# One pass over the attention scores, staggered merging, and a re-ordered set of queues in a two-block float32 transformer kernel

## The chip, the cores and the metric
The kernel runs on one core of one Trainium2 chip. The metric is device time in microseconds (us) from the start to the end of one execution; the median of the runs is what counts.

## The reference
A sequence of 512 tokens with 1024 channels passes two models, one after the other, in float32. The first has two layers, each with a mixer and a gated MLP with a causal convolution of width 3, each half with a norm before and a norm behind, and with shift, scale and gate columns from a modulation vector (`mod = silu(c) @ mod_w[l]`, six pieces of 1024 for each layer). The mixer of layer 0 is a convolution block (two products, a depthwise convolution of width 31, a LayerNorm over channels and a swish). That of layer 1 is differential attention:

```python
s = q . k * scale + bias;  s = where(rel >= 0, s, -inf);  p = softmax(s)      # for both halves c of a head
a = p[:, :, 0] - lam * p[:, :, 1];  o = a @ v
o = rms_norm(o, subln_g) * (1 - lambda_init);  y = o.reshape(S, 1024) @ w_o
```

The second model has one block: an input product to all of the attention inputs and gates, a sparse attention (an indexer picks 128 keys for a query; 8 heads share k and v), a second causal attention from low-rank latents (8 heads, rotary part of 32), two branch products merged with gates, `x + merged @ w_out`, and an MLP with a squared relu, then a final norm.

## The kernel before
Every large product is done as three float32r products (`mm3`, L204 to L207): high part by high part, low by high, high by low. So each piece of weights that comes from DRAM (`wr`) is cast by ScalarE to its high part (`wh`, L137), and the low part is a subtraction (`wl`, L139) on VectorE or, where `b.lo_pool` says so, on GpSimd; `LO_POOL` gives every how many-th piece by stage. Activations are split likewise (`hh`, `hl`, L350 and L351). Tokens lie in 4 tiles of 128 (`tok`); a transposition of a tile is 8 products of 128x128 (`transp`, L334).

Each engine runs its instructions in the order of the code. `Builder.ahead(n)` loads and splits the next n pieces (`la` pieces split ahead, `ld` loaded ahead), `get` takes one, and `tick` takes one step of a background generator, above all of `mod_chunk` (L243: 8 multiply-adds of 128x1024, called macc, for one piece of `mod`; then products with ones, L259 for columns or L266 for broadcast rows). `HELD` names pieces whose last part is done at a fixed later place.

The places that the change touches, in order of the program:
- **Start** (`keep_busy`, `m_pe`, loop over `k` at L840 to L884). Products by 128 columns `hh` with `w1` (L859) alternate with one-column products for the first `mod` columns (L744). `h_evac` (L772, L773) makes `hh` of the next step from a transposition and the `mcol` columns (L279).
- **LayerNorm** before `w2` (`ln_tok`, L978 to L1006): `ln_norm` (L969) makes `zn`, `ln_put` the transposition and its evacuation (L976). `down8` (L461 to L501) is a product with a 1024x1024 matrix for 4 token tiles, in 2 halves of 8 steps each, with the norm chain of a tile (`chain`) put between the steps of the next.
- **MLPs of the first model**: `run_ffn` starts the background list `bg`.
- **Attention of layer 1**: `proj(hd)` makes q and k of a head (`kq`, L1192 to L1194). An item is a head and a query tile `(hd, qb)`, with n = 128(qb+1) keys. `attn1_s` (L1197 to L1235) does two score products (`sc`, c = 0, 1), then on VectorE a maximum of the part without bias (L1213), an add-and-maximum of the last 256 columns with the bias (L1214), then on ScalarE an exp of each part (L1220, L1222), and sums and differences in `comb` (L1229 to L1233). `attn1_t` transposes the weights (`aT`, L1241), `attn1_v` multiplies with v (L1249) and writes `o` (L1251). When head 7 of a tile is done, GpSimd raises 8 columns to the power -1/2 (L195) and VectorE scales all of `o` (L1302, 128x1024); the scaled tile is transposed for `wo`'s `down8`, which runs among the last items and behind them. `MULT` and `AGE` count items until the scaling and the transposition.
- **Second block**: the input projection (units, rope on 32 rows, `kh`), the indexer's selection, and the items of both attentions (`mla_s` L1574 to L1603, `dsa_s` L1605 to L1620), with gate units and branch-b units as fillers between items. `cmaj` (L1666 to L1673) turns a finished tile to channels for the branch product. `LALD2` is set by `deeper()` before the first branch-b unit.
- **Merge** (L1721 to L1732): 8 branch-a units; after each second one the pair of gates is added (L1729), halved and split (`mgh` L1730, `mgl` L1731); then `wout` by `down8`.

## Time and profile before

| | us |
|---|---|
| median of 3 runs (lowest, highest) | 2028.94 (2028.92, 2034.42) |
| the profiled execution | 2029.45 |
| its span in the trace | 2027.7 |
| TensorE (PE) busy | 1960.3, 97% |
| VectorE (DVE) busy | 1258.3, 62% |
| ScalarE (ACT) busy | 827.6, 41% |
| GpSimd (POOL) busy | 138.7, 7% |
| mean granted TensorE clock | 0.988 |

A share of busy time is a mean over stages; the time of a program like this is lost where PE waits. The timeline of PE has 53 waits of 0.15 us or more. Two kinds of loss can be read: a wait itself, in brackets behind an instruction with what ended it, and a stretch in which the granted clock is at the lower of its two levels (1.2 GHz instead of 2.4), which the view by windows shows as PEclk near 0.5.

### The profile page before, as it was taken

How to read it: one execution, taken by the hardware profiler on the slowest of the kernel's cores; microseconds unless marked ns; L12 is line 12 of the kernel's file. 1: busy time of each engine (PE TensorE's matmuls, PEld its weight loads, DVE VectorE, ACT ScalarE, POOL GpSimd, SP SyncE). 2: the span in 40 equal slices, each digit the busy share in tenths (PEclk: the TensorE clock that was granted, in tenths of full speed). 3: DMA queues.
4: the chain of work that ended last, by engine and by line, in shares of the span. 5: the costliest groups of instructions: out<-in, count | busy, mean ns of one | idle time of the engine just before them, and what ended most of it. 6: DMA issues, size and time to landing. Idle time of an engine off the chain costs nothing. (4 is left out here: it accounts for less than half of the span.)

```text
span 2027.7 us, 25858 instructions
## 1 busy us (share of the span) xinstructions
PE 1960.3 (97%) x9722; PEld 1616.4 (80%) x9725; DVE 1258.3 (62%) x2406; ACT 827.6 (41%) x1675; POOL 138.7 (7%) x99
## 2 busy tenths in 40 slices
PE   9999999999999999889999999998999999999998
PEld 6889788777887877678888887867777878888887
DVE  5779677777855565767666623678686746433432
ACT  3312454443424456744444413554445435322421
POOL 1001000000000111210000000122212100000000
PEclk8999999999999999999999999999999999999999
DMA  9455146434675211312932323311114442332221
GB/s 358 133 206 196 74 151 224 156 125 138 244 265 175 82 46 64 142 59 92 256 104 84 125 73 137 121 57 53 42 52 130 152 161 90 124 125 84 82 94 42
DMA packets 85417, 259.47 MB, mean 128 GB/s; under 512 B 9429, under 2 KB 21117, under 8 KB 85290
## 3 DMA queue, kind: packets, MB, share of 16 engines
q1 hardware_dynamic: 77802, 232.63, 34.1%
q10 hardware_dynamic: 7488, 25.17, 3.3%
q8 instruction: 76, 1.25, 0.3%
q14 instruction: 51, 0.42, 0.1%
HBM read 243.04 MB, written 23.64 MB: 132 GB/s over the span
## 5 line engine op out<-in xcount | busy, mean ns | idle before, releaser
L205 PE MATMUL up<-hh,wh 128*128 128x512 f32 (+1 forms) x1232 | 456.4, 370 | 3.4 <-ACT wh L137 1.7
L207 PE MATMUL up<-hh,wl 128*128 128x512 f32 (+1 forms) x1232 | 453.8, 368 | 4.0 <-DVE wl L139 3.9
L206 PE MATMUL up<-hl,wh 128*128 128x512 f32 (+1 forms) x1232 | 452.6, 367 | 0.2
L139 DVE TENSOR_TENSOR wl<-wr,wh 128x1024 fp32r<-128x1024 f32 (+2 forms) x257 | 311.8, 1224 | 174.1 <-ACT wh L137 146.7
L137 ACT CAST wh<-wr 128x1024 fp32r<-128x1024 f32 (+2 forms) x308 | 307.9, 1019 | 183.1 <-DMA wr<-in_w_all_dram 99.8
L207 PEld LDWEIGHTS up<-hh,wl 128*128 128x128 f32 x1232 | 232.0, 188 | 47.5 <-DVE wl L139 9.2
L205 PEld LDWEIGHTS up<-hh,wh 128*128 128x128 f32 x1232 | 232.0, 188 | 46.2 <-ACT wh L137 3.5
L206 PEld LDWEIGHTS up<-hl,wh 128*128 128x128 f32 x1232 | 232.1, 188 | 40.2 <-issue 1.5
L205 PE MATMUL acc<-wh,ih 128*128 128x512 f32 x608 | 237.4, 390 | 0.0
L206 PE MATMUL acc<-wl,ih 128*128 128x512 f32 x608 | 236.8, 389 | 0.2 <-DVE wl L139 0.2
L207 PE MATMUL acc<-wh,il 128*128 128x512 f32 x608 | 236.7, 389 | 0.0
L139 POOL TENSOR_TENSOR wl<-wr,wh 128x1024 fp32r<-128x1024 f32 (+1 forms) x51 | 108.0, 2125 | 975.3 <-ACT wh L137 912.2
L206 PEld LDWEIGHTS acc<-wl,ih 128*128 128x128 f32 x608 | 114.1, 188 | 24.3 <-DVE wl L139 0.9
L207 PEld LDWEIGHTS acc<-wh,il 128*128 128x128 f32 x608 | 114.1, 188 | 23.8
L205 PEld LDWEIGHTS acc<-wh,ih 128*128 128x128 f32 x608 | 114.1, 188 | 23.6
L243 DVE SCALAR_TENSOR_TENSOR macc<-mraw,cact,macc 128x1024 f32<-128x1024 f32 x74 | 95.4, 1289 | 6.6 <-DMA mraw<-in_mod_w_dram 6.0
L1071 ACT CAST ih<-fc 128x512 fp32r<-128x512 f32 x44 | 37.9, 860 | 142.5 <-DVE fc L1063 142.5
L1039 ACT ACTIVATE fc<-up,cols 128x512 f32<-128x512 f32 x88 | 68.2, 775 | 36.0 <-PE up L207 36.0
L1044 DVE SCALAR_TENSOR_TENSOR fc<-up,cols,fc 128x384 f32<-128x384 f32 (+3 forms) x176 | 72.7, 478 | 4.1 <-ACT fc L1039 4.1
L205 PE MATMUL unit<-hh,wh 128*128 128x512 f32 x152 | 72.7, 479 | 0.7 <-ACT kh L1448 0.6
L1055 ACT ACTIVATE fc<-fc 128x512 f32<-128x512 f32 x44 | 27.8, 632 | 102.6 <-DVE fc L1044 61.6
L1072 DVE TENSOR_TENSOR il<-fc,ih 128x512 fp32r<-128x512 f32 x44 | 39.8, 904 | 40.8 <-ACT ih L1071 40.8
(336 smaller groups left out, 3110.3 us busy)
## 6 DMA issues: line engine op xcount, KB each, us to landing
wr<-in_w_all_dram SPq DMA_DIRECT2D x282, 512.0 KB, 3.7
mraw<-in_mod_w_dram SPq DMA_DIRECT2D x80, 512.0 KB, 4.9
xd<-x ACTq DMA_DIRECT2D x20, 512.0 KB, 2.6
x<-xd ACTq DMA_DIRECT2D x20, 512.0 KB, 5.8
mraw<-in_w_all_dram SPq DMA_DIRECT2D x16, 512.0 KB, 9.6
wr<-in_w_all_dram SPq DMA_DIRECT2D x17, 256.0 KB, 2.6
wr<-in_w_all_dram SPq DMA_DIRECT2D x8, 384.0 KB, 8.8
sk<-fd SPq DMA_DIRECT2D x6, 512.0 KB, 15.7
```

The costliest lines, as they stand in the source:

```text
L137: self.nc.scalar.copy(hi, raw)
L139: (self.nc.gpsimd if pool else self.nc.vector).tensor_tensor(out=lo, in0=raw, in1=hi, op=ALU.subtract)
L205: mm(ps, lh, rh, start=start, stop=False)
L206: mm(ps, lh, rl, start=False, stop=False)
L207: mm(ps, ll, rh, start=False, stop=stop)
L243: nc.vector.scalar_tensor_tensor(out=acc, in0=raws[k], scalar=s, in1=acc, op0=ALU.mult, op1=ALU.add)
L1039: nc.scalar.activation(out=o, in_=ps, func=AF.Identity, scale=dw[:, 88 + j:89 + j], bias=dwb[:, j:j + 1])
L1044: nc.vector.scalar_tensor_tensor(out=a, in0=e, scalar=dw[:, w + j:w + j + 1], in1=a, op0=ALU.mult, op1=ALU.add)
L1055: nc.scalar.activation(out=o, in_=o, func=AF.Silu)
L1071: nc.scalar.copy(hi, o)
L1072: nc.vector.tensor_sub(lo, o, hi)
```

## The change
1. **One pass over scores.** The bias tiles of attention 1 become [128, 512] for a head, zero in the first half; the add-and-maximum runs over all n columns, the maximum of the unbiased part is gone, and one exp serves a half of the item instead of two. The second block's causal attention does the same with a wide mask. The order lists have 65 instructions less on VectorE and 64 less on ScalarE.
2. **LO_POOL** goes from (2, 0, 2, 1, 0) to (0, 0, 0, 1, 0): 15 low parts in the stage of w_v and attention 1 and 6 in the second block's input projection go from GpSimd to VectorE. The eight rope copies to `kh` on GpSimd become four on VectorE.
3. **End of attention 1.** Heads 6 and 7 go query tile by query tile. Six heads of a tile are scaled when head 6 is done (128x768), the last two at age 1 (128x256). Within `wo` the norms' roots are taken on GpSimd (`power_on`) and not by ScalarE's Sqrt.
4. **Constant first products**: the last parts of three pieces of `mod` (m14, m13, m15: two times 8 one-column products for each of 2 parts, and 2 products with ones) go from the first MLP's down stage to fillers behind `proj(7)`.
5. **LayerNorm**: the transposition of tile 0 is put before the norm of tile 1; tiles 2 and 3 and the transposition of tile 1 go to step 5 of `w2`'s `down8`.
6. **Start**: `WARM` (32, 5) becomes (38, 2), with one more warm product after each 4 of the first group; for k = 0 `ahead(2)` moves behind `h_evac(1)`.
7. **PAUSE**: six empty ticks before the background list in both MLPs of the first model.
8. **Second block**: other `SEL_RATE`; `cmaj` of the causal attention at age 5 instead of 3; each bias load of the sparse attention one item earlier; `la`, `ld` grow by one for each branch-b unit; the merge's low part is issued behind the next unit, its last pair is merged singly; `wout`'s first tile does k < 6 of both halves first; `reload` one tile at a time.

```diff
-LO_POOL = (2, 0, 2, 1, 0)
+LO_POOL = (0, 0, 0, 1, 0)
-MULT = 4
+MULT = (1, 1, 1, 1)
-AGE = (9, 11, 6, 10, 14, 12, 21, 12)
-SEL_RATE = (1.4, 1, 0.6, 0.4, 1.0, 1.3, 1.3, 1.0, 1.2)
+AGE = (7, 11, 6, 8, 12, 12, 21, 12)
+SEL_RATE = (1.0, 1.4, 0.6, 0.4, 1.0, 1.3, 1.3, 1.0, 1.2)
-HELD = [(0, 2), (0, 4)]
-WARM = (32, 5)
+HELD = [(0, 2), (0, 4), (1, 4), (1, 3), (1, 5)]
+WARM = (38, 2)
+PAUSE = 6
...
@@ rstd2
-        if self.phase:
+        if self.phase or self.power_on:
...
@@ down8
+            cut = 0 if tok else last
+            todo = [(half, k) for half in range(2) for k in range(8 - cut)]
+            todo += [(half, k) for half in range(2) for k in range(8 - cut, 8)]
...
@@ start
-    for _ in m_pe(*START_GROUPS[0]):
-        pass
+    for i, _ in enumerate(m_pe(*START_GROUPS[0])):
+        if i % 4 == 3:
+            keep_busy(idle, 1)
...
-        b.ahead(2)
+        if k:
+            b.ahead(2)
...
             lo_k = h_evac(k + 1, h_t(k + 1))
+        b.ahead(2)
...
@@ ln_tok
+            ln_put(0)
             ln_norm(1)
-            ln_put(0)
...
-            ln_norm(2)
-            ln_put(1)
-            b.reload()
-            ln_norm(3)
...
+        if i == 5:
+            ln_next()
...
@@ run_ffn
-        b.bg += bg
+        b.bg += [('pause', iter(range(PAUSE)))] + bg
...
@@ attn1_s
-            if nf:
-                nc.vector.reduce_max(m[:, c:c + 1], sc[c][:, :nf], axis=AX.X)
-            nc.vector.tensor_tensor_reduce(out=pt[:, c, nf:n], in0=sc[c][:, nf:n], in1=bts, scale=1.0,
...
+            nc.vector.tensor_tensor_reduce(out=pt[:, c, :n], in0=sc[c][:, :n], in1=bt[hd][:, 512 - n:], scale=1.0,
+                                           scalar=-3.0e38, op0=ALU.add, op1=ALU.max, accum_out=m[:, c:c + 1])
...
+            nc.scalar.activation(out=pt[:, c, :n], in_=pt[:, c, :n], func=AF.Exp, bias=nm[:, c:c + 1],
+                                 accum_out=tot[:, c:c + 1])
...
@@ done
+        if hd == 5:
+            orr[tok] = b.rstd_pool(oss[tok][:, 0:6], 128, 6)
+        if hd == 6:
+            scale_heads(tok, 0, 6)
...
-        orr[tok] = b.rstd_pool(oss[tok], 128, 8)
+        orr[tok] = b.rstd_pool(oss[tok][:, 6:8], 128, 2)
...
-    fillers = [proj(hd) for hd in range(1, 8)]
+    fillers = [proj(hd) for hd in range(1, 8)] + [b.held.pop(tag) for tag in ('m14', 'm13', 'm15')]
...
@@ second: fillers, merge, wout
-    def deeper():
-
-        b.la, b.ld = LALD2
-        yield
-    fillers.append(deeper())
+    def branch_unit(j):
+
+        b.la, b.ld = min(LALD2[0], LALD[0] + 1 + j), min(LALD2[1], LALD[1] + 1 + j)
+        yield from unit_gen(('br', 'b', j), yb, branch_b(j), nk=4)
...
-            if age[kt] == 3:
+            if age[kt] == (5 if kt[0] == 'm' else 3):
...
+        if low:
+            low()
+            low = None
+        if j >= 6:
+            low = merge(3, j - 6, j - 5)
+        elif j % 2:
+            low = merge(j // 2)
...
+    for i, _ in enumerate(b.down8(mg, 'wout', (add0, chain3), T, E3, last=2)):
+        if 6 <= i < 10:
+            b.reload(i - 6)
```

**Where the order moves.** VectorE at the start, from the low part of `h` at step k = 0 to the first multiply-add of step 1 (before; then the change). `wl` is the low part of a weight piece, `mcol` the modulation columns that `hh` of step 1 needs:

```order
L774 TENSOR_TENSOR hl_95<-hf_230,hh_91 128x512
L733 SCALAR_TENSOR_TENSOR macc_233<-mraw_118,cact_87,macc_233 128x128 x4
L139 TENSOR_TENSOR wl_244<-wr_120,wh_243 128x768
L139 TENSOR_TENSOR wl_264<-wr_130,wh_263 128x768
L279 TENSOR_TENSOR mcol_99<-ps_268,cols_72 128x1
L281 SCALAR_TENSOR_TENSOR mcol_99<-mcol_99,cols_72 128x1
L279 TENSOR_TENSOR mcol_100<-ps_268,cols_72 128x1
L731 TENSOR_SCALAR macc_294<-mraw_126,cact_87 128x256
```

```order
L783 TENSOR_TENSOR hl_95<-hf_237,hh_91 128x512
L742 SCALAR_TENSOR_TENSOR macc_240<-mraw_118,cact_87,macc_240 128x128 x4
L141 TENSOR_TENSOR wl_251<-wr_120,wh_250 128x768
L284 TENSOR_TENSOR mcol_99<-ps_271,cols_72 128x1
L286 SCALAR_TENSOR_TENSOR mcol_99<-mcol_99,cols_72 128x1
L284 TENSOR_TENSOR mcol_100<-ps_271,cols_72 128x1
L141 TENSOR_TENSOR wl_298<-wr_130,wh_297 128x768
L740 TENSOR_SCALAR macc_301<-mraw_126,cact_87 128x256
```

The second of the two subtractions stood ahead of the three `mcol` instructions; now it stands behind them.

VectorE at the end of attention 1, from the last half of `wo`'s first tile to the scaling of the last tile of `o` (before):

```order
L378 TENSOR_TENSOR y_7281<-acc_7220,gbc_3356 128x512
L292 TENSOR_SCALAR sm_7283<-ssn_88 128x1
L298 RECIPROCAL sm_7285<-sm_7284 128x1
L382 SCALAR_TENSOR_TENSOR x_7026<-y_7234,sm_7285,x_7026 128x512
L382 SCALAR_TENSOR_TENSOR x_7026<-y_7281,sm_7285,x_7026 128x512
L292 TENSOR_SCALAR sm_7293<-ssx_89 128x1
L298 RECIPROCAL sm_7295<-sm_7294 128x1
L309 TENSOR_SCALAR xr_7299<-x_7026,sm_7295 128x1024
L1302 TENSOR_TENSOR o_5550<-o_5550,sm_7247 128x1024
L350 CAST hh_7018<-hf_7332 128x2x128
```

The same end in the change, first the scaling of the last two tiles, then the norm chain:

```order
L355 CAST hh_6946<-hf_7159 128x2x128
L356 TENSOR_TENSOR hl_6950<-hf_7159,hh_6946 128x2x128
L1293 TENSOR_TENSOR o_5527<-o_5527,sm_7146 128x256
L375 TENSOR_TENSOR y_7177<-acc_7063,gbc_3519 128x512
L1293 TENSOR_TENSOR o_5528<-o_5528,sm_6885 128x768
L355 CAST hh_6943<-hf_7207 128x2x128
```

```order
L383 TENSOR_TENSOR y_7222<-acc_7133,gbc_3519 128x512
L297 TENSOR_SCALAR sm_7224<-ssn_88 128x1
L299 TENSOR_SCALAR sm_7226<-ssn_88,sm_7224 128x1
L387 SCALAR_TENSOR_TENSOR x_6951<-y_7177,sm_7226,x_6951 128x512
L387 SCALAR_TENSOR_TENSOR x_6951<-y_7222,sm_7226,x_6951 128x512
L297 TENSOR_SCALAR sm_7234<-ssx_89 128x1
L299 TENSOR_SCALAR sm_7236<-ssx_89,sm_7234 128x1
L314 TENSOR_SCALAR xr_7240<-x_6951,sm_7236 128x1024
L1293 TENSOR_TENSOR o_5528<-o_5528,sm_7263 128x256
L375 TENSOR_TENSOR y_7177<-acc_7243,gbc_3519 128x512
```

The scaling of tile 3 stood whole behind the first tile's norm chain and its `xr`; now 768 of its 1024 columns stand ahead of the chain, and 256 are left behind `xr`.

ScalarE in the sparse attention at the first branch-b units: `p` is an item's exp, `oa` the evacuation of its result, `hf` the copy of a `cmaj` transposition, `wh` a weight cast (before; then the change):

```order
L1618 ACTIVATE p_14177,sm_14185<-p_14177,sm_14184 128x256
L137 CAST wh_14190<-wr_13799 128x512
L137 CAST wh_14194<-wr_14004 128x512
L137 CAST wh_14200<-wr_14198 128x512
L137 CAST wh_14206<-wr_14204 128x512
L137 CAST wh_14212<-wr_14210 128x512
L137 CAST wh_14218<-wr_14216 128x512
L1669 COPY hf_14238<-ps_14233 128x512
L1635 ACTIVATE oa_13828<-pv_14247,sm_14085 128x64
L1618 ACTIVATE p_14251,sm_14259<-p_14251,sm_14258 128x256
```

```order
L1630 ACTIVATE p_13968,sm_14008<-p_13968,sm_14007 128x256
L139 CAST wh_14013<-wr_13645 128x512
L139 CAST wh_14017<-wr_13849 128x512
L1647 ACTIVATE oa_13673<-pv_14034,sm_13893 128x64
L1630 ACTIVATE p_14000,sm_14046<-p_14000,sm_14045 128x256
L1681 COPY hf_14064<-ps_14059 128x512
L1647 ACTIVATE oa_13673<-pv_14073,sm_13930 128x64
L1630 ACTIVATE p_14038,sm_14085<-p_14038,sm_14084 128x256
```

Six casts in a row stood between an item's exp and the `cmaj` copy; two are left, and another item's evacuation and exp pass between them and the copy.

## Rows read from the trace of the kernel before

**Rows 1.** The page: busy us of each engine, its share of the span, instructions.

```profile
PE 1960.3 (97%) x9722; PEld 1616.4 (80%) x9725; DVE 1258.3 (62%) x2406; ACT 827.6 (41%) x1675; POOL 138.7 (7%) x99
```

**Rows 2.** Windows by stage: length, then busy us (instructions) by engine, clock, DMA.

```profile
370.00:540.00 170.00, 164.12 (x705) 129.13 (x703) 130.22 (x194) 70.68 (x87) 0.00 (x0) 1.00 0.46 157
700.00:830.00 130.00, 128.40 (x643) 96.11 (x642) 78.69 (x257) 78.26 (x261) 19.16 (x8) 1.00 0.17 55
830.00:885.00 55.00, 40.05 (x219) 31.40 (x219) 43.35 (x117) 35.44 (x112) 15.50 (x11) 0.97 0.32 122
1300.00:1400.00 100.00, 90.59 (x419) 72.41 (x419) 69.94 (x137) 47.14 (x84) 25.20 (x17) 0.97 0.18 56
1400.00:1470.00 70.00, 66.28 (x322) 52.97 (x321) 52.72 (x186) 31.95 (x99) 18.61 (x10) 0.98 0.15 47
```

**Rows 3.** Windows on stretches with PE at the low clock; columns as in the last.

```profile
28.10:41.80 13.70, 13.70 (x50) 12.17 (x51) 7.13 (x19) 2.20 (x4) 0.95 (x1) 0.50 1.03 406
...
195.40:202.20 6.80, 6.08 (x19) 4.55 (x19) 6.46 (x20) 5.93 (x14) 0.13 (x1) 0.51 0.42 150
...
1542.20:1547.00 4.80, 4.80 (x15) 3.81 (x16) 3.02 (x14) 3.13 (x10) 0.67 (x1) 0.50 0.14 44
...
1625.50:1629.00 3.50, 3.33 (x7) 2.19 (x8) 2.56 (x3) 1.05 (x1) 0.00 (x0) 0.52 0.98 323
```

**Rows 4.** Timelines of PE and ACT, 20 to 31 us: start, duration, instruction [idle before <-releaser].

```profile
26.80 0.50 PE L859 MATMUL up<-hh,wh 128*128 128x512 f32 x1 [2.07 <-DMA mraw<-in_w_all_dram]
...
23.71 0.83 ACT L137 CAST wh<-wr 128x768 fp32r<-128x768 f32 x1 [5.41 <-DMA wr<-in_w_all_dram]
```

**Rows 5.** Timelines of PE and DVE, 190 to 198 us.

```profile
190.98 1.84 PE L259 MATMUL ps<-ones,macc 128*128 128x1 f32 x16
...
196.12 1.94 PE L334 MATMUL ps<-ident,zn 128*128 128x128 f32 x8 [1.99 <-DVE zn L969]
...
195.56 1.38 DVE L969 TENSOR_SCALAR zn<-z,mv,sm 128x256 f32<-128x256 f32 x4 [0.98 <-POOL sm L195]
```

**Rows 6.** The page: costliest groups; busy us, mean ns | idle before, releaser.

```profile
L243 DVE SCALAR_TENSOR_TENSOR macc<-mraw,cact,macc 128x1024 f32<-128x1024 f32 x74 | 95.4, 1289 | 6.6 <-DMA mraw<-in_mod_w_dram 6.0
```

**Rows 7.** Groups by form, 700 to 880 us, DVE and ACT; columns as in the last.

```profile
L1213 DVE TENSOR_REDUCE sm<-sc 128x1 f32<-128x256 f32 x16 | 6.7, 422 | 10.8 <-PE sc L1203 10.8
...
L1220 ACT ACTIVATE p<-sc,sm 128x256 f32<-128x256 f32 x16 | 7.5, 467 | 14.2 <-DVE sm L1229 12.4 <-PE kp L207 1.0 <-DVE sm L1230 0.7
```

**Rows 8.** Groups by form: DVE from 640 to 900 us, then POOL over the span.

```profile
L139 DVE TENSOR_TENSOR wl<-wr,wh 128x1024 fp32r<-128x1024 f32 x16 | 22.9, 1434 | 7.5 <-ACT wh L137 7.4
```

```profile
L139 POOL TENSOR_TENSOR wl<-wr,wh 128x1024 fp32r<-128x1024 f32 x36 | 88.5, 2459 | 902.8 <-ACT wh L137 844.4 <-issue 19.3 <-ACT o L1251 13.0
```

**Rows 9.** Timelines of DVE, ACT and PE, 826 to 884 us.

```profile
849.20 2.00 DVE L1232 SCALAR_TENSOR_TENSOR sm<-sm,sm,nlam 128x1 f32<-128x1 f32 x1
...
876.95 1.22 DVE L1302 TENSOR_TENSOR o<-o,sm 128x1024 f32<-128x1024 f32 x1
...
871.57 1.28 ACT L297 ACT_TABLE_LOAD   x1 [0.95 <-DVE sm L292]
...
878.32 1.94 PE L334 MATMUL ps<-ident,o 128*128 128x128 f32 x8 [4.40 <-DVE o L1302]
```

**Rows 10.** Timeline of DVE, 1328 to 1386 us.

```profile
1340.54 0.69 DVE L1479 TENSOR_TENSOR sw<-sw,trig 128x512 f32<-128x512 f32 x1
1341.15 2.87 DVE L1480 TENSOR_TENSOR sw<-sw,trig 128x512 f32<-128x512 f32 x1
```

**Rows 11.** Timelines of ACT, DVE and PE, 1530 to 1545 us.

```profile
1533.12 3.21 ACT L137 CAST wh<-wr 128x512 fp32r<-128x512 f32 x6
...
1537.82 1.32 DVE L1672 TENSOR_TENSOR yal<-hf,yah 128x256 fp32r<-128x256 f32 x1
...
1542.20 0.80 PE L205 MATMUL unit<-ybh,wh 128*128 128x512 f32 x1 [3.87 <-DVE sm L1615]
```

**Rows 12.** Timeline of PE, 1614 to 1632 us.

```profile
1625.50 0.66 PE L205 MATMUL acc<-wh,mgh 128*128 128x512 f32 x1 [4.25 <-ACT mgh L1730]
```

More of the change, by code (lines that the diff above doesn't have):

```diff
@@ L186, in finish @@
                 pass
+        for _ in self.held.pop(tag, ()):
+            pass
     def col(self, name):
@@ L320, in rows, with reload @@
         return src[tok * 128:tok * 128 + 128, :]
-    def reload(self):
-        for tok in range(NT):
+    def reload(self, only=None):
+        for tok in range(NT) if only is None else (only,):
             if self.x[tok] is None:
@@ L459, in down, with down8 @@
         chain[1](3, ps[3])
-    def down8(self, act, key, chain, T, E, bias=None, pre=None):
+    def down8(self, act, key, chain, T, E, bias=None, pre=None, last=0):
         nc = self.nc
@@ new lines, in down8 @@
+            todo = [(half, k) for half in range(2) for k in range(8 - cut)]
+            todo += [(half, k) for half in range(2) for k in range(8 - cut, 8)]
+            for half, k in todo:
+                if k == 0:
+                    ps.append(self.PS(n="acc"))
+                    if bias is not None:
+                        for i, bt in enumerate(bias):
+                            nc.tensor.matmul(ps[half], self.ones1r, bt[:, half * 512:half * 512 + 512], start=i == 0, stop=False)
+                w = ws[half * 4 + k // 2]
+                self.mm3(ps[half], act.hi(k, a, b), act.lo(k, a, b), w[0][:, k % 2, :], w[1][:, k % 2, :],
+                         k == 0 and bias is None, k == 7)
+                if k % 2 and not half and not tok:
+                    ws.append(self.get((key, 1, k - 1)))
+                if k == 1 and half == 1 and tok >= 2:
+                    self.ahead(min(la, tok - 1))
+                if k == (6 if cut else 3) and half == 1:
+                    chain[0](tok, ps[0])
+                if k == 5 and half == 1 and tok:
+                    T(tok - 1)
+                    E(tok - 1)
+                if k == 7:
+                    self.tick(rate)
+                else:
+                    yield
@@ L1144, in program @@
     sk1, tab = b.rb
-    b.finish('m15')
+    for tag in ('m14', 'm13', 'm15'):
+        while any(e[0] == tag for e in b.bg):
+            b.tick(1)
     hkv, hq = holder['kv'], b.newpair(8)
@@ L1277, in program @@
     todo = [(hd, qb) for hd in range(6) for qb in range(4)]
-    todo += [(6, 0), (6, 1), (7, 0), (6, 2), (7, 1), (6, 3), (7, 2), (7, 3)]
+    todo += [(hd, qb) for qb in range(4) for hd in (6, 7)]
     sg = b.C([128, 1], n="sg")
@@ L1715, in second @@
     pipeline(todo, s_of, lambda kind, hd, qb, pt: att_t(hd, qb, *pt), v_of, fill, done, LAG)
-    while fillers or any(age[kt] < 3 for kt in age):
+    while fillers or any(age[kt] < 5 for kt in age):
         advance()
@@ L1750, in E3 @@
         b.evac_gain(tp.pop(tok), tok, holder['h3'], mlg)
-    b.reload()
-    for _ in b.down8(mg, 'wout', (add0, chain3), T, E3):
-        pass
+    for i, _ in enumerate(b.down8(mg, 'wout', (add0, chain3), T, E3, last=2)):
+        if 6 <= i < 10:
+            b.reload(i - 6)
     if stop == 'attn2':
```

141 lines of the change are left out of this document (57 added, 84 removed).

## The prediction
> **What bounds the kernel now.** I read the busy times first, then PE's timeline with its waits, then windows by stage, and last the timelines of the engines that end a wait. PE is busy for 1960.3 us of the 2027.7 us span, VectorE for 1258.3 [rows 1]: over the whole, PE bounds, and the change takes no product away (it adds seven short warm-up ones). So what it can gain lies in two places. One is PE's idle time, 2027.7 - 1960.3 = 67.4 us, which sits in a few stages: 5.9 us of 170 in the first MLP's weight-bound part, 15.0 of 55 at the end of attention 1, 9.4 of 100 in the second block's input projection, 3.7 of 70 in the items of the second causal attention [rows 2]. The other is the low clock: behind several waits PE runs at 1.2 GHz instead of 2.4, for 13.7 us at the start, 6.8 in the LayerNorm, 4.8 in the sparse attention, 3.5 in the merge [rows 3]. The same products at 2.4 GHz would need half of that, so each stretch costs half its length. A wait that goes can take such a stretch with it. I sum against the profiled execution, 2029.45 us, which is 0.5 above the median of the runs. A measurement of this kernel can tell 0.3%, or 6 us, from no change.
>
> **Part by part (gain in us; in brackets the ends).**
>
> *Start.* PE waits 2.07 us at 26.80 [rows 4]. The row names a DMA, but the wait's last link is `hh` of step 1. It needs `mcol`, which stands on VectorE behind the second subtraction, and that one waits for a cast that itself waited for its weights until 23.71 [rows 4]. In the change `mcol` and `hh` stand ahead of that cast and that subtraction, so `hh` is ready some 2 us earlier and the wait should go. Behind it lie 13.7 us at 1.2 GHz, worth 6.85 [rows 3]. Upper end 2.07 + 6.85 = 8.9, lower end 0, since the DMA share is 1.03 through the stretch [rows 3] and the weights of the next steps may then be late instead. I take **5**.
>
> *LayerNorm.* PE waits 1.99 at 196.12, for `zn` of tile 1, which waited on GpSimd's root [rows 5], and the clock is low for 6.8 us, worth 3.4 [rows 3]. In the change the bias and the products with tile 0 need only tile 0's transposition, and the second tile's eight transpositions come later under products. Upper end 5.4; lower end 1, if VectorE's `hh` and `hl` of tile 0, now issued ahead of tile 1's `zn` at 1.38 for four [rows 5], only shift the wait. I take **4**.
>
> *Pauses in the MLPs.* Three multiply-adds of 1.29 [rows 6] leave VectorE's queue in the stage where PE waits 5.9 us in all for casts and subtractions [rows 2]: at most 3 x 1.29 = 3.9, at least 0 (they come back later, where VectorE has room). I take **2**.
>
> *One pass over scores.* PE idles only 1.6 us of 130 there [rows 2], so this is mostly cover. VectorE loses 16 maxima of 0.42 and as many shorter ones, ScalarE 32 exps of some 0.47 with what belongs to them [rows 7]; VectorE gets 15 subtractions at 1.22 to 1.43 [rows 8], some 20 us over 190. With 78.7 busy of 130 before [rows 2], PE's products hide that. I take **1** (0 to 1.6).
>
> *End of attention 1.* 15.0 us idle [rows 2]. The last transposition of `o` waits 4.40 for a scaling of 1.22 that stands behind the norm chain of `wo`'s first tile, in which ScalarE loads a table for 1.28 [rows 9]. In the change 768 of 1024 columns are scaled before that chain, the rest costs about a third of 1.22, and the table load is gone. The `mod` products moved here take 1.84 for one set of eight [rows 5], so two sets and the two products with ones are about 5.5 us of PE work that needs no late operand. That work only changes its place; what it gains is the waits that it fills. Against it: two GpSimd powers a tile instead of one, and two more a tile for `wo`'s norms. I replayed the two orders with these durations: the waits shrink to about 5, of which some 3 are for the first tile's evacuation behind the scaling and the subtraction on VectorE. So 15 - 5 = **10** (4 to 13).
>
> *Input projection.* PE idles 9.4 us [rows 2]. VectorE gets 6 subtractions, 6 x 1.22 = 7.3, and four copies of 32x1024 that no row shows; the nearest row is 0.69 for 512 columns [rows 10], so 0.7 to 1.4 each, and I take 1.4, or 5.5 in all. What it gets back: while GpSimd subtracts, operations on VectorE stretch, 2.87 against 0.69 for the same shape one row before [rows 10]. Those are gone with the GpSimd work, about 4 us in all, and its chain to the indexer no longer waits behind a 2.46 us GpSimd subtraction [rows 8]. I take **2** (-6 to 6). The Trainium skill, GPSIMD Engine Reference, section Key points, says that GpSimd shares its SBUF interfaces with VectorE, to the harm of instructions with two SBUF inputs; the 2.87 us row agrees. By that rule the move alone gives back every stretched row, which would be the upper end.
>
> *Second causal attention.* 3.7 us idle [rows 2]. With one exp and no maximum the chain of an item is about 0.5 to 0.9 shorter (0.42 and 0.47 in attention 1 [rows 7]), and `cmaj` has two more items to be ready. I take **3** (0 to 4).
>
> *Sparse attention.* PE waits 3.87 for a release by VectorE, which was busy with `cmaj` parts at 1.32 each, behind ScalarE's copy, behind six casts in a row of 3.21 us [rows 11]; 4.8 us at the low clock follow, worth 2.4 [rows 3]. In the change `la` grows by one, so the row of six is two. Upper end 3.87 + 2.4 = 6.3, lower end 2, since VectorE's parts are still stretched while GpSimd subtracts there (that entry of LO_POOL stays). I take **5.5**.
>
> *Merge.* PE waits 4.25 for the last pair's high part [rows 12], and 3.5 us at the low clock follow [rows 3]: 4.25 + 1.75 = 6.0. In the change six steps of both halves, 12 x 3 products of about 0.23, stand ahead of the last pair, some 8 us; that covers the chain. I take **5** (2 to 6).
>
> Sum: 5 + 4 + 2 + 1 + 10 + 2 + 3 + 5.5 + 5 = 37.5. For waits that form anew, above all at the powers and at later table loads, I take off 3. So 2029.45 - 34.5 = 1994.95, or about 1994.5 against the median. All upper ends give 1974, all lower ones about 2026; taken as independent their half widths add to about 10, so the likeliest case alone has 1982 to 2008.
>
> **Rivals.**
> *The clock stays low.* The waits go, but not the low stretches. For it: in the 13.7 us at the start PE is busy for 13.70 of 13.70 and the clock is 0.50 to the end [rows 3], so closing a wait need not lift it. Against it: in the other places the clock falls at the wait. The Trainium skill, TensorE: Matmul & The Clock Gate, section What's actually happening, says that the clock follows how busy PE has lately been; the row at the start does not agree, if busy is what the profile calls busy. Clock terms in my sum are about 3, 2.5, 2 and 1.5, so about 9 or 10 are lost: 2004.
>
> *Waits come back in the same places.* One chain ends a few hundred nanoseconds behind the one removed, and half of each gain stays: -17, or 2012. For it: many engines are within a microsecond of each other at the end of attention 1 and in the projection.
>
> *GpSimd's powers hold VectorE.* A one-column operation took 2.00 us at 849.20, longer than the scaling of 1024 columns at 1.22 [rows 9], while GpSimd was at work. If each of some 16 powers in the end of attention 1 does that to a scaling or a norm step, the 10 of that part go: 2005.
>
> *VectorE becomes the bound (slower).* The place is the stage of w_v and attention 1 and the input projection; the mechanism is that 21 subtractions stand in VectorE's queue ahead of an item's maximum or a rope step. The price is 21 x 1.22 + 5.5 = 31.1, all on the path. Against that stand the parts elsewhere, 37.5 - 1 - 10 - 2 - 3 = 21.5, so +9.6, or about 2039. It decides from the point at which VectorE has no idle time left between items; with 51 of 130 us idle there before [rows 2] it is far off in attention 1 and near only in the projection.
>
> **How the numbers follow.** Forecast 0.50; low clock 0.18; waits come back 0.17; powers 0.09; VectorE bound 0.06. The range takes the likeliest case and reaches over the next two to 2013; at the low end it goes to 1980. Faster than -6 us: all but the last case and the tail of the second and third, 0.89. Slower: 0.05. Between: 0.06.
>
> **What would show it.** Right: no PE wait over 1 us at `hh` of step 1, and a shorter low stretch before 42 us; the products of `w2` running on behind eight transpositions; one PE wait of about 3 us in the end of attention 1 where there were a dozen; no row of six casts before a `cmaj` copy; `wout` without a wait at `mgh`. Wrong: a low stretch of the same length at the start; VectorE over 90% busy in the input projection with PE waiting there for 15 us or more; a wait at `o` or `xr` of 4 us as before; bias loads of the sparse attention that end a wait.

## The result, and the profile after
The change runs in 2005.42 us (median of 4 runs, 2004.52 to 2005.96); the ratio to the kernel before, whose four runs beside these took 2028.92 to 2034.51 (median 2031.68), is 0.987, with a 95% interval of 0.9851 to 0.989. The profiled execution's span is 2003.2 us against 2027.7, so 24.5 us are to be found. The prediction had 34.5, with 1980 to 2013 as the range: the sign holds, the time lies in the range, and the size was seven tenths of the forecast. By its number alone the result lies nearer to two rivals (2004 and 2005) than to the forecast of 1994.5; which of them were at work is read below, stage by stage.

The page after, busy time, and then windows on the same stages as [rows 2], each shifted by what the program had gained until there. Line numbers from here on are those of the changed kernel: L209 to L211 are the three products, L139 is the cast of a weight piece, L141 its subtraction, L355 the cast to `hh`.

```profile
PE 1955.5 (98%) x9729; PEld 1614.1 (81%) x9732; DVE 1245.2 (62%) x2341; ACT 812.5 (41%) x1555; POOL 91.8 (5%) x90
```

```profile
364.50:534.50 170.00, 164.10 (x704) 129.07 (x703) 130.81 (x193) 69.50 (x86) 0.00 (x0) 1.00 0.46 158
689.30:819.30 130.00, 129.31 (x654) 97.26 (x652) 73.62 (x228) 72.78 (x212) 0.00 (x0) 1.00 0.20 62
818.70:873.70 55.00, 46.86 (x252) 36.30 (x252) 39.65 (x112) 32.41 (x96) 11.44 (x18) 0.91 0.33 120
1288.70:1388.70 100.00, 91.48 (x422) 73.34 (x422) 74.44 (x156) 49.78 (x90) 10.21 (x5) 0.97 0.18 55
1386.60:1456.60 70.00, 66.10 (x322) 53.82 (x321) 47.38 (x152) 27.42 (x67) 18.79 (x10) 0.95 0.16 46
```

PE's idle time fell from 67.4 to 47.7 us, 19.7 of the 24.5; its busy time fell by 4.8 although it has a few products more. The stretches at the low clock within the span sum to 50.4 us before and 44.5 after, so at half their length they are worth 2.9 of the 4.8; the rest is not traced here. The end of attention 1 (third row) has 46.86 busy of 55 where it had 40.05, but its clock is 0.91 where it was 0.97. The first MLP (first row) has not changed. The low clock, in the same view:

```profile
16.20:26.40 10.20, 10.18 (x38) 8.40 (x37) 4.71 (x15) 3.49 (x5) 0.00 (x0) 0.51 1.03 408
33.40:40.20 6.80, 6.80 (x24) 5.80 (x23) 4.43 (x14) 2.17 (x3) 0.95 (x1) 0.51 1.03 406
842.50:849.30 6.80, 4.38 (x12) 3.56 (x13) 5.49 (x15) 5.10 (x13) 0.93 (x2) 0.50 0.28 90
1419.40:1426.20 6.80, 6.20 (x17) 4.75 (x18) 3.64 (x16) 4.30 (x10) 0.00 (x0) 0.50 0.00 0
```

At the start there are 17 us at the low clock, as many as before (3.4 and 13.7 there). Those in the LayerNorm, the sparse attention and the merge [rows 3] are gone in this profile, a new one of 3.4 us stands at 822 us, and two of 6.8 us stand at the two longest waits of the new program (at the second, the kernel before had 3.4):

```profile
844.91 0.80 PE L209 MATMUL acc<-wh,hh 128*128 128x512 f32 x1 [5.93 <-DVE hh L355]
...
1420.00 0.76 PE L209 MATMUL unit<-hh,wh 128*128 128x512 f32 x1 [3.90 <-DVE p L1639]
```

A stage's length is read from PE's timeline, from one mark to the next. This table is worked out so, by the first or last product or transposition of a kind. The start ends at the first convolution product (`zp`); the LayerNorm begins at the first transposition of `zn`, and w2 ends at the last transposition of `xr`; the first MLP goes from there to the next one of `xr`. Attention 1 goes from the first to the last product of the q and k projections, its end from there to the last transposition of `xr` in `wo`'s norm. The input projection goes from the first transposition of `xr` behind the second MLP to the first one of attention weights; the second causal attention from there to its last score products; the sparse attention to the last transposition of `oa`; and the last stage to the first transposition of `xr` behind `wout`. "Moved" is PE work of the constant first products that changed its stage (by run 5, 3.6 us out of the first MLP and 1.8 out of the stage behind it; their sum, 5.4, goes into the end of attention 1). Each column is one profile, and what that can hide is said behind run 1.

| stage | before | after | gain, moved work taken out | forecast |
|---|---|---|---|---|
| start, to 92 us | 92.24 | 90.59 | 1.65 | 5 |
| LayerNorm and w2 | 72.39 | 68.55 | 3.8 | 4 |
| first MLP | 368.91 | 365.50 | -0.2 | 2 |
| attention 1, to the last projection | 130.34 | 129.40 | 0.9 | 1 |
| end of attention 1, wo | 91.25 | 91.81 | 4.9 | 10 |
| input projection | 115.93 | 113.71 | 2.2 | 2 |
| second causal attention | 120.56 | 120.44 | 0.1 | 3 |
| sparse attention, to its last copy | 82.59 | 75.00 | 7.6 | 5.5 |
| branch a, merge, first tile of wout | 57.26 | 54.59 | 2.7 | 5 |
| all else | | | 0.9 | -3 |

### The profile page after: what moved, and what is told of

It is laid out like the page before. It is cut to its first block, busy times and chain, and to the rows that moved or that the text cites. A ratio compares the mean times of both kernels' runs of the same rounds, so it can differ in the third digit from the quotient of the medians.

```text
span 2003.2 us, 25577 instructions
## 1 busy us (share of the span) xinstructions
PE 1955.5 (98%) x9729; PEld 1614.1 (81%) x9732; DVE 1245.2 (62%) x2341; ACT 812.5 (41%) x1555; POOL 91.8 (5%) x90
## 4 chain that ended last, share of the span: by engine, by line
PE 43%; DVE 4%; ACT 2%; issue 1%; DMA 0%; DVEq 0%; ACTq 0%; SPq 0%
PE up L210 5%; PE up L209 5%; PE up L211 5%; PE acc L210 5%; PE acc L211 5%; PE acc L209 5%; PE unit L209 2%; PE unit L211 2%; PE unit L210 2%; PE pv L1646 2%; PE sc L1592 1%; PE aT L1636 1%; DVE wl L141 1%; DVE qs L1398 0%; PE ps L339 0%
## 5 line engine op out<-in xcount | busy, mean ns | idle before, releaser
L211 PE MATMUL up<-hh,wl 128*128 128x512 f32 (+1 forms) x1232 | 454.0, 369 | 4.5 <-DVE wl L141 4.5
L209 PE MATMUL up<-hh,wh 128*128 128x512 f32 (+1 forms) x1232 | 456.0, 370 | 1.7 <-ACT wh L139 1.4
L141 DVE TENSOR_TENSOR wl<-wr,wh 128x1024 fp32r<-128x1024 f32 (+3 forms) x278 | 333.0, 1210 | 169.3 <-ACT wh L139 157.5
L139 ACT CAST wh<-wr 128x1024 fp32r<-128x1024 f32 (+2 forms) x308 | 307.4, 1019 | 163.1 <-PE acc L210 45.0
L211 PEld LDWEIGHTS up<-hh,wl 128*128 128x128 f32 x1232 | 231.9, 188 | 48.3 <-DVE wl L141 10.1
L209 PEld LDWEIGHTS up<-hh,wh 128*128 128x128 f32 x1232 | 232.0, 188 | 44.1 <-ACT wh L139 3.2
L209 PE MATMUL acc<-wh,ih 128*128 128x512 f32 x608 | 237.1, 390 | 0.0
L211 PE MATMUL acc<-wh,il 128*128 128x512 f32 x608 | 236.6, 389 | 0.0
L211 PEld LDWEIGHTS acc<-wh,il 128*128 128x128 f32 x608 | 114.1, 188 | 23.7
L209 PEld LDWEIGHTS acc<-wh,ih 128*128 128x128 f32 x608 | 114.1, 188 | 23.6
L209 PE MATMUL unit<-hh,wh 128*128 128x512 f32 x152 | 73.0, 480 | 4.0 <-DVE p L1639 3.9
L1760 DVE TENSOR_TENSOR x<-x,acc 128x512 f32<-128x512 f32 x24 | 16.5, 686 | 95.0 <-PE acc L211 95.0
L141 POOL TENSOR_TENSOR wl<-wr,wh 128x1024 fp32r<-128x1024 f32 (+1 forms) x30 | 56.5, 1893 | 299.3 <-ACT wh L139 247.3
```

Of the source, the lines that this page charges most:

```text
L139: self.nc.scalar.copy(hi, raw)
L141: (self.nc.gpsimd if pool else self.nc.vector).tensor_tensor(out=lo, in0=raw, in1=hi, op=ALU.subtract)
L209: mm(ps, lh, rh, start=start, stop=False)
L211: mm(ps, ll, rh, start=False, stop=stop)
```

## The experiments
Each of these kernels but the last ran once. The change lies between 2004.5 and 2006.0 in its four runs, but the last kernel spreads over 4.8 us in five runs and the kernel before over 5.7 in nine, so one total can't tell a difference of less than some 5 us. A stage that is the same in many profiles can tell far less: the sparse attention took 75.00 us in all eleven profiles that leave it as it is. All edits are made to the changed kernel.

**1. The old warm-up.**
```diff
-WARM = (38, 2)
+WARM = (32, 5)
-        if i % 4 == 3:
-            keep_busy(idle, 1)
```


> The change with its old warm-up (32 and 5 warm products, none between the first one-column products); the new place of the casts at step 0 stays. Theory: the new warm-up is what makes PE run the first 10 us of products at the low clock (5.1 us lost from 16 to 27 us in the change's trace, 1.7 in the kernel before), so with the old one step 0 runs at full clock, step 1 follows without a wait, and the program is 1 to 4 us faster than the change: 2001 to 2004. Rival 1: the weights and the modulation rows from DRAM set the pace, step 1 waits for them and nothing is gained: 2005. Rival 2: the stretch before 42 us grows back to 13.7 us and takes what the first one gives: 2004 to 2006.

2004.29 us, but not for the reason given: the stage up to the mark at 92 us took 93.48, 2.9 longer than in the change's profile, with the clock low from 12.8 to 29.9 us. What is gained lies in stages that the edit doesn't touch.

```profile
12.50:29.50 17.00, 16.78 (x67) 14.78 (x68) 6.61 (x18) 4.74 (x7) 0.09 (x1) 0.51 1.03 410
```

The theory falls: the old warm-up does not keep the clock up here. How much of the 2.9 us is the edit's is open, as the next paragraph says: it is 1.5 more than the slowest of eleven profiles of the new start.

**What eleven profiles of one start say.** In the eleven profiled kernels with the change's own start (its own profile, and those of runs 2 to 8 and 10 to 12) this stage took 88.2 to 92.0 us, 90.0 in the mean, with the same instructions in the same order. The low stretches lie at 14 to 28 us in some, at 16 to 27 and 33 to 41 in others, at 20 to 24 and 30 to 38 in others still. So the kernel before, with 92.24 in its one profile, lies at the upper edge, about 2 us above the mean. That would be the 2.07 us wait that went, but one profile can't show it. The twelve profiles with the new LayerNorm order show the same in its stage: 30.5 us to w2's first norm in eight, 33.6 in four, and there the clock is low with PE never idle:

```profile
192.00:202.20 10.20, 10.20 (x38) 8.76 (x37) 8.66 (x20) 3.26 (x5) 0.00 (x0) 0.54 0.16 51
```

That is run 3's; in the change's own profile the clock is 1.00 from 188 to 198 us. Other stages vary in the same way: the end of attention 1 took 89.6 to 93.4 us in the eight profiles of its order.

**2. GpSimd's subtractions back.**
```diff
-LO_POOL = (0, 0, 0, 1, 0)
+LO_POOL = (2, 0, 2, 1, 0)
```


> The change with LO_POOL = (2, 0, 2, 1, 0): the 21 subtractions go back to GpSimd, the rope copies stay on VectorE. Theory: the move is worth about 2 us in the input projection, where GpSimd's work stretched VectorE's, and nothing in attention 1: 2006 to 2009, with operations of 1.8 to 2.9 us on VectorE again in the projection. Rival (VectorE is the bound there): taking 7 to 18 us off VectorE makes it faster: 2000 to 2004.

2007.30 us. The input projection took 116.68 us against 113.71, attention 1 up to its last projection 129.39 against 129.40; the other stages stay within the spread that the profiles of one code have (below run 1). As expected: the move is worth 3.0 us in the projection and nothing in attention 1, and the stretched operations of [rows 10] are back, with the same numbers:

```profile
1330.00 2.83 POOL L141 TENSOR_TENSOR wl<-wr,wh 128x1024 fp32r<-128x1024 f32 x1 [6.10 <-ACT wh L139]
```

```profile
1330.51 2.87 DVE L1494 TENSOR_TENSOR sw<-sw,trig 128x512 f32<-128x512 f32 x1
...
1334.79 0.47 PE L209 MATMUL uk<-cknh,wh 128*128 128x512 f32 x1 [2.78 <-DVE iw L1567]
```

The 2.87 us ends within 0.6 us of GpSimd's subtraction, at 1333 us. In the change no subtraction is on GpSimd there, and the same instruction reads:

```profile
1329.05 0.68 DVE L1494 TENSOR_TENSOR sw<-sw,trig 128x512 f32<-128x512 f32 x1
```

That VectorE would be the bound there is refuted.

**3. The jump of la and ld back.**
```diff
-        b.la, b.ld = min(LALD2[0], LALD[0] + 1 + j), min(LALD2[1], LALD[1] + 1 + j)
+        b.la, b.ld = LALD2
```
(set once ahead of the first branch-b unit)

> The change with the jump of la and ld before the first branch-b unit. Theory: the row of casts ahead of the sparse attention's first copy to channels comes back, and with it a wait of about 4 us and a low stretch that loses 2 to 3.4: 2010 to 2013. Rival: the wait went because VectorE's parts or the bias loads moved: 2005 to 2007.

2008.61 us, between the two expectations; the sparse attention took 80.18 us against 75.00, branch a and the merge 0.6 more, which is within their spread (54.6 to 56.3 us). The row of casts and the wait are those of [rows 11]:

```profile
1515.61 3.21 ACT L139 CAST wh<-wr 128x512 fp32r<-128x512 f32 x6
...
1524.75 0.50 PE L209 MATMUL unit<-ybh,wh 128*128 128x512 f32 x1 [3.93 <-DVE sm L1627]
```

The theory holds for the wait. Of the stage's 7.6 us gain this one line makes 5.2; the other 2.4 are not shown by a run.

**4. la left at 7 in the merge.**
```diff
-        b.la = min(LALD2[0], 12 - j)
```


> The change with la left at 7 in the merge. Theory: the two waits of 1.69 and 0.82 for the last cast and subtraction of wout's first pieces come only from the lowered la, and go: 2002.5 to 2004. Rival: the casts and subtractions now stand ahead of the last pair's high and low parts, and the wait comes back there, 2 to 4 us: 2005 to 2008.

2007.26 us, and the rival is right. One wait of 1.69 goes, and one of 0.53 becomes 3.19, for the last pair but one's low part, since the extra cast and subtraction stand ahead of it:

```profile
1597.08 0.50 PE L209 MATMUL acc<-wh,mgh 128*128 128x512 f32 x1 [0.29 <-ACT mgh L1739]
1601.01 0.50 PE L211 MATMUL acc<-wh,mgl 128*128 128x512 f32 x1 [3.19 <-DVE mgl L1740]
1610.49 0.50 PE L210 MATMUL acc<-wl,mgh 128*128 128x512 f32 x1 [0.76 <-DVE wl L141]
```

In the change the same place reads:

```profile
1598.37 0.50 PE L209 MATMUL acc<-wh,mgh 128*128 128x512 f32 x1 [0.30 <-ACT mgh L1739]
1599.63 0.50 PE L211 MATMUL acc<-wh,mgl 128*128 128x512 f32 x1 [0.53 <-DVE mgl L1740]
1603.88 0.49 PE L209 MATMUL acc<-wh,mgh 128*128 128x512 f32 x1 [1.69 <-ACT wh L139]
1605.19 0.50 PE L210 MATMUL acc<-wl,mgh 128*128 128x512 f32 x1 [0.82 <-DVE wl L141]
```

So four short waits, 3.3 us in sum, stand where one of 4.25 and one of 0.17 stood. In this profile no low stretch follows them, and the stage took 54.59 us. But of the twelve profiles that leave the merge as it is, eight have one of 3.4 us there, and these took 56.0 to 56.3 us; run 6's:

```profile
1603.40:1606.80 3.40, 3.40 (x10) 2.61 (x8) 1.90 (x2) 0.20 (x1) 0.00 (x0) 0.51 0.97 372
```

Against the 57.26 of the kernel before the merge thus gains 2.7 us in some executions and 1.1 in most.

**5. Constant first products back in the MLP's down stage.**
```diff
-HELD = [(0, 2), (0, 4), (1, 4), (1, 3), (1, 5)]
+HELD = [(0, 2), (0, 4)]
-    fillers = [proj(hd) for hd in range(1, 8)] + [b.held.pop(tag) for tag in ('m14', 'm13', 'm15')]
+    fillers = [proj(hd) for hd in range(1, 8)]
```


> The change with the constant first products (m14, m13, m15) where the kernel before has them. Theory: in the end of attention 1 they fill waits; without them the waits there come back by 3 to 5 us and the first MLP with the stage behind it is 5.5 us longer, so the end of attention 1 ends 0 to 2.5 us sooner after its start and the whole is 3 to 5.5 us slower: 2008 to 2011. Rival: they only change place, PE time is the same: 2004.5 to 2006.5.

2006.12 us: the rival. The MLP and the stage behind it grow by 3.63 and 1.78, the end of attention 1 shrinks by 5.86; the move gives nothing that this profile can tell. In the change's profile a low stretch of 3.4 us, worth 1.7, lies at 822 us among the moved products, and run 5 has none there; but runs 1 and 10 have the moved products without it (89.6 us instead of 91.8), and against those the move would gain 1.8. The waits of the end of attention 1, the 5.94 us one too, are the same with and without it, so these products do not stand where the waits are.

**6. No pauses, and the old selection rates.**
```diff
-PAUSE = 6
+PAUSE = 0
-SEL_RATE = (1.0, 1.4, 0.6, ...
+SEL_RATE = (1.4, 1, 0.6, ...
```


> Two edits in two stages, told apart by stage: PAUSE = 0, and the old SEL_RATE (1.4, 1.0 for the first two groups of items). Theory: the pauses gain nothing, the stage from 260 to 625 us keeps its length within 0.5 us; the old rate takes selection steps from VectorE's queue ahead of the copy at 1419 us, so the wait of 3.9 us and its low stretch go and the second causal attention is 3 to 5 us shorter: 2000 to 2002. Rivals: the pauses gain 2 us as forecast, the first stage grows by 2; the wait at 1420 comes from GpSimd's subtraction beside the copy to channels and stays: 2005 to 2007.

2004.44 us. The MLP took 364.92 against 365.50 and w2's stage ahead of it 0.6 more, so the pauses only move 0.6 us from one stage to the next. The second causal attention took 118.40, where seven of the nine unedited profiles of it have 117.5 to 118.2 and two, the change's own and run 9's, have 120.4. So the rates give no gain in the stage's length that these profiles can tell. Yet they have a part in the wait at 1420. With the old ones no selection step stands between the copy's casts and `p` (run 12 shows the steps of the change), and the wait is 2.55 instead of 3.90:

```profile
1417.49 0.40 DVE L1639 COPY p<-aT 128x256 f32<-128x256 f32 x1
```

```profile
1418.04 0.67 PE L1592 MATMUL sc<-kh,qh 96*128 96x256 f32 x2 [2.55 <-DVE p L1639]
```

The two long profiles have a low stretch of 3.4 us at the stage's start and one of 6.8 at the wait. Run 6 has the first, and only 3.4 us at the wait; of the seven short ones none has the first. So what the rates are worth depends on which of these the run is set against.

**7. An earlier evacuation of the first tile.**
```diff
-AGE = (7, 11, 6, 8, 12, 12, 21, 12)
+AGE = (5, 11, 6, 8, 10, 12, 21, 12)
```


> The change with AGE 5 and 10 instead of 7 and 12 for wo's first tile: its transposition and evacuation stand ahead of the last item's score pass and exps, not behind. Theory: the 5.9 us wait for the first hh is a matter of that order; PE goes on about 4 us sooner and the low stretch behind it shortens by 1.7: 1999 to 2002. Rival: VectorE's whole work in these 12 us is the limit, the wait comes back at the last items' transpositions: 2004 to 2006.

2005.55 us, the rival's range; the end of attention 1 and wo took 89.89 us against 91.8, so 1.9 of the 4 expected. The wait for `hh` is 0.18 instead of 5.93, and two others have taken most of its place:

```profile
839.31 0.44 PE L339 MATMUL ps<-ident,o 128*128 128x128 f32 x2 [1.50 <-DVE o L1293]
841.92 0.50 PE L209 MATMUL acc<-wh,hh 128*128 128x512 f32 x1 [0.18 <-DVE hh L355]
847.86 1.09 PE L1247 MATMUL aT<-ident,p 128*128 128x128 f32 x4 [2.46 <-DVE p L1239]
```

By the waits both readings have a share: the order cost 2 us of the 5.9, and VectorE's work in these 12 us the rest. But the MLP behind is 1.5 us longer here (349.82 against 348.30), with a low stretch of 3.4 us at 909 us that the change's profile has not:

```profile
909.00:912.40 3.40, 3.40 (x17) 3.40 (x18) 3.21 (x5) 3.40 (x9) 0.00 (x0) 0.51 0.49 159
```

So 0.4 us are left of the 1.9. Run 12, with the same edit, has that stretch too, but so have runs 2 and 5 without it, so that the edit brings it is not shown.

**8. The two-part score pass back.**
```diff
-            nc.vector.tensor_tensor_reduce(out=pt[:, c, :n], in0=sc[c][:, :n], in1=bt[hd][:, 512 - n:], ...
+            if nf:
+                nc.vector.reduce_max(mf[:, c:c + 1], sc[c][:, :nf], axis=AX.X)
+            nc.vector.tensor_tensor_reduce(out=pt[:, c, nf:n], in0=sc[c][:, nf:n], in1=bt[hd][:, 512 - n + nf:], ...
...
+                nc.scalar.activation(out=pt[:, c, :nf], in_=sc[c][:, :nf], func=AF.Exp, ...
```
(and in `mla_s` likewise)

> The change with the two-part score pass of before in attention 1 and in the second causal attention (maximum of the unbiased part, two exps for a half), all else as changed. Theory: in the body of attention 1 PE's products hide it (within 1 us from 690 to 812 us), in its end and in the second causal attention it costs 1 to 2 us each: 2006 to 2009. Rival (the one pass is the main gain): 2012 to 2020.

2012.10 us, the lower end of the rival's range: by this one total the one pass is worth some 7 us, by the stages below 5.3 to 8.2, more than expected and at most a third of the gain. The body of attention 1 is 0.8 longer, its end 3.1, the second causal attention 1.4 to 4.3 (against 120.4 or 117.6). In the end, the waits for an item's weights, for `o` and for `hh` grow:

```profile
837.28 0.52 PE L1258 MATMUL aT<-ident,p 128*128 128x128 f32 x3 [2.01 <-DVE p L1250]
840.63 0.44 PE L339 MATMUL ps<-ident,o 128*128 128x128 f32 x2 [0.51 <-DVE o L1304]
849.20 0.79 PE L209 MATMUL acc<-wh,hh 128*128 128x512 f32 x1 [7.36 <-DVE hh L355]
```

So the one pass, which the prediction priced at 1 in the body, is worth most where projections no longer cover it.

**9. The cast of step 0 first.**
```diff
-        if k:
-            b.ahead(2)
+        b.ahead(2)
```
(and without the one behind `h_evac`)

> The change with the second cast and subtraction of step 0 back ahead of step 1's columns and hh; the new warm-up stays. Theory: this order is what took the 2.07 us wait away, so at step 1 a wait of 1 to 2 us is back where step 0 runs at full clock, and the stage up to 90 us is about 2 us longer than the 88.3 to 92.0 us that it took in the runs with the changed order. Rival: where step 0 runs at the low clock it lasts 3.5 us longer anyway, the cast's weights have landed by then, and the order makes no difference: no wait at step 1.

2006.61 us, and no wait at step 1: the rival. The stage took 90.81, inside the spread of the changed order; step 0 ran at the low clock from 14 to 28 us and lasted longer than the cast needed. What the order is worth at the full clock was not seen again. The traces do show what it does: in the twelve profiles of the new order `hh` of step 1 is done 1.9 us behind the start of its transposition, in the kernel before 5.4 and in run 9 2.4. The products between that transposition and step 1 took 3.4 us at the full clock in the kernel before, so 1.9 would leave no wait there either; that is an estimate.

**10. The old LayerNorm order.**
```diff
-            ln_put(0)
             ln_norm(1)
+            ln_put(0)
...
+            ln_norm(2)
+            ln_put(1)
+            b.reload()
+            ln_norm(3)
...
-        if i == 5:
-            ln_next()
```


> The change with the LayerNorm order of before (all norms and both transpositions ahead of w2). Theory: the 2 us wait for zn of tile 1 comes back, with a low stretch behind it; the stage up to w2's first norm takes 33.5 to 36 us instead of the 30.5 of most runs. Rival: the low stretch at 191 to 203 us, which three of the ten runs had in the changed order too (33.6 us), has nothing to do with the order, and the stage takes 30.5 to 32.5.

2004.00 us, though the stage took 33.65 us instead of 30.56 with the wait and the low stretch of [rows 3, 5]:

```profile
194.25 1.94 PE L339 MATMUL ps<-ident,zn 128*128 128x128 f32 x8 [1.99 <-DVE zn L981]
```

The theory holds for the place. But four of the twelve profiles of the new order took 33.6 us as well, so by these profiles, of which two have the old order (this one and the kernel before, 33.7), the new order is worth 3.1 us in most executions and nothing in some. The total is lower because this run lost nothing at 822 us and less at 1420.

**11. No subtraction on GpSimd in the second block.**
```diff
-LO_POOL = (0, 0, 0, 1, 0)
+LO_POOL = (0, 0, 0, 0, 0)
```


> The change with every subtraction on VectorE, also the 30 that it left on GpSimd from 1370 to 1570 us. Theory: beside them VectorE's operations stretch (2.15 us for a cast of 0.29 at 1413), and that cast stands in the chain to the 3.9 us wait at 1420; without them the wait falls to about 2 and the second causal attention is 1.5 to 3 us shorter: 2001 to 2004. Rival (VectorE has no room here): 15 subtractions of 1.22 and 15 of 0.7 on an engine that is busy for three quarters of the time bring new waits: 2006 to 2015.

2022.81 us: the rival, beyond its upper end. The edit moves 29 of the 30; one, at 162 us, stays on GpSimd. The second causal attention took 128.87 us, the sparse one 82.40, with waits like these:

```profile
1412.05 0.50 PE L209 MATMUL unit<-hh,wh 128*128 128x512 f32 x1 [1.66 <-DVE sm L1597]
1426.91 0.77 PE L209 MATMUL unit<-hh,wh 128*128 128x512 f32 x1 [3.19 <-DVE p L1639]
```

Here VectorE sets the time, and GpSimd's stretching of it is the smaller cost.

**12. Both placements together.** The chain to the wait at 1420, in the change: GpSimd's subtraction, VectorE's cast for the copy to channels beside it, for which VectorE had waited 2.15 us, then two rounds of selection steps (L1550, L1551), and the release of a bank by `p` (L1639) behind them:

```profile
1413.29 2.38 POOL L141 TENSOR_TENSOR wl<-wr,wh 128x1024 fp32r<-128x1024 f32 x1 [9.14 <-ACT wh L139]
```

```profile
1413.67 2.15 DVE L1683 CAST ybh<-hf 128x256 fp32r<-128x256 f32 x1 [2.15 <-ACT hf L1681]
1415.92 0.43 DVE L1684 TENSOR_TENSOR ybl<-hf,ybh 128x256 fp32r<-128x256 f32 x1
1416.26 0.29 DVE L1683 CAST ybh<-hf 128x256 fp32r<-128x256 f32 x1
...
1417.00 0.56 DVE L1550 MAX8 sm<-wk 128x8 f32<-128x384 f32 x1
...
1418.91 0.54 DVE L1551 MATCH_REPLACE8 wk<-sm,wk 128x384 f32<-128x384 f32 x1
...
1419.44 0.41 DVE L1639 COPY p<-aT 128x256 f32<-128x256 f32 x1
```

```diff
-AGE = (7, 11, 6, 8, 12, 12, 21, 12)
+AGE = (5, 11, 6, 8, 10, 12, 21, 12)
-            if age[kt] == (5 if kt[0] == 'm' else 3):
+            if age[kt] == (6 if kt[0] == 'm' else 3):
```


> The change with AGE 5 and 10 for wo's first tile, and the second causal attention's copy to channels one step later (age 6 instead of 5). Theory: the first edit is worth 1.9 us in the end of attention 1, as in the look before; the second takes the copy's first cast out of the time of GpSimd's subtraction at 1413 us, so that the wait of 3.9 us at 1420 shrinks by 1 to 2 and its low stretch with it: 2001.5 to 2004 by the median. Rival 1: the clock's stretches shift and give back what the waits give: 2004.5 to 2006. Rival 2: the copy, one step later, meets the selection's steps instead, and the wait stays.

1998.00 us (median of 5 runs, 1996.04 to 2000.85), ratio to the kernel before 0.9847 with 0.9833 to 0.986: faster than was expected, and all five runs lie below the four of the change, though these were not taken beside them. The second causal attention took 114.08 us, 6.4 less than in the change's profile, 3.5 less than in most and 4.1 less than in run 7, which has the first edit alone. The first edit again gives 1.9 in the end of attention 1 and loses 1.5 in the MLP behind it, so nearly all of the gain is the later copy's. What happened is a little different from the theory:

```profile
1412.05 0.41 DVE L1639 COPY p<-aT 128x256 f32<-128x256 f32 x1
1412.37 1.54 DVE L1683 CAST ybh<-hf 128x256 fp32r<-128x256 f32 x1
```

The cast still stretches beside GpSimd's subtraction (1.54), but `p` now stands ahead of it. The longest PE wait near there is 0.95 us, and no low stretch follows.

## Why the prediction was right or wrong, point by point
- **Where the time is.** Right: 19.7 of the 24.5 us are PE waits, about 2.9 the low clock, and no product was saved. Of the sum's 37.5 us some 9 were clock terms, so 6 of the 10 us that are missing are low stretches that stayed or moved. To that extent the rival "the clock stays low" held, and that its 2004 was so near is partly luck, since the waits fell short as well.
- **Start.** The failing step is "behind it lie 13.7 us at 1.2 GHz, worth 6.85", of which I counted about 3. The wait went; the low stretches only moved, 17 us of them before and after, and they move from run to run. The prediction had named a stretch of the same length at the start as a sign of being wrong. The rival "the clock stays low" was right here and wrong at the sparse attention, where none of eleven profiles has a low stretch left; in the LayerNorm four of twelve and in the merge eight of twelve still have one.
- **LayerNorm.** Right in mechanism, and 3.8 for 4 in this profile. Run 10 gives 3.1 of it back with the wait; most of the other 0.7 are the pauses' (run 6). And a third of the profiles had the low stretch without a wait, so that the size came out is in part luck.
- **Pauses.** The step "three multiply-adds leave VectorE's queue in the stage where PE waits" failed: the waits for casts and subtractions are the same, 5.9 us, and run 6 loses 0.6 in w2's stage and gains it back in the MLP.
- **Attention 1's body.** Right: 0.9 for 1. The price of the pass lay elsewhere (run 8).
- **End of attention 1.** "The waits shrink to about 5" is where it failed, by 5 us. They are 8.1 of 55 us, 5.93 in one, and 6.8 us at the low clock lie at that one, which I hadn't put in. The scaling of 768 columns and a subtraction stood ahead of the last item's score pass, and the first tile's evacuation behind its exps. And the moved products filled no wait (run 5: the same waits without them). No run undoes the earlier scaling, the order of the items or the powers by themselves, so the 4.9 that were gained are not split among them.
- **Input projection.** Right: 2.2 for 2, and 3.0 when the subtractions alone are undone. The four copies took 0.69 each and not the 1.4 that I put in without a row. The Trainium skill, GPSIMD Engine Reference, section Key points (its interfaces are shared with VectorE, to the harm of instructions with two SBUF inputs), agrees in direction: 2.87 against 0.69. It does not decide where to put the work: run 11 took 29 more subtractions off GpSimd, and with them the sharing in the attentions, and lost 17 us. And the stretched cast at 1413 us has one input, of float32, which that sentence covers only by its other clause, an instruction in a mode that uses both ports; that the cast ran in such a mode no run shows.
- **Second causal attention.** The term was 3 and the profile had 0.1; seven of nine profiles of the same code had 117.5 to 118.2 us, which against the one profile of the kernel before would be 2.4 to 3.0. So the size of this term is not settled. The chain of an item did get shorter (run 8). What stood against it: the copy to channels at age 5 ran beside a GpSimd subtraction, and with two selection rounds behind it held back a bank's release. One step later it gives 6.5 in all (run 12); without the selection rounds the wait there is 2.55 and not 3.90 (run 6).
- **Sparse attention.** Right in mechanism, 7.6 for 5.5, over my upper end of 6.3: the whole stretch of 6.8 us at the low clock went, not only the 4.8 behind the wait.
- **Merge.** Half of it or less (2.7 in this profile, 1.1 in most): the wait of 4.25 became four that sum to 3.3, as the pair's chain is now in several links. What I had not priced is that casts of later weight pieces stand behind the last high part (1.69). No run undoes the merge or the new order of `wout` by itself, so the gain is read from the waits alone.
- **GpSimd's powers.** Wrong as a rival: they took 1.3, 0.7 and 0.6 us, and no PE wait in the end of attention 1 ends with one. The 2.00 us row at 849.20, from which I priced it, doesn't speak of a power at all: it lies beside a subtraction on GpSimd, in the kernel before:

```profile
848.82 2.36 POOL L139 TENSOR_TENSOR wl<-wr,wh 128x1024 fp32r<-128x1024 f32 x1 [1.19 <-ACT wh L137]
```

## What to carry to other kernels
Where five queues run in program order, price a moved operation by what stands behind it in its queue until the next instruction that another engine waits for: a one-step shift of a 2 us cast was worth 3.5 to 6.4 us, as much as most terms of this change. Work that only fills time helps if it stands at the wait, and not somewhere in the stage. A stage's length in one profile can be a matter of where the low-clock stretches fall; take several profiles of one code before a difference of 3 us is put down to an edit, and look whether a gain in one stage comes back as a loss in the next.

## What the runs showed that was not expected
The low clock came without a wait: PE was busy for 10.20 of 10.20 us while the clock was 0.54 in the LayerNorm stage of run 3, and at 1.00 in the same instructions of the change's own profile. What PE did before the fall was, in both, transpositions and one-column products. The Trainium skill, TensorE: Matmul & The Clock Gate, section What's actually happening, lets the clock follow how busy PE has been; the rows here do not agree, if busy is the profile's busy time. Why the same order falls in one execution and not in the next is left open.
